# First query tile ahead of two value tiles, attention outputs split at their store

## The chip, the cores and the metric

The kernel runs on one core of a Trainium2 chip. A core has five engines that matter here, each working through its own instruction queue in order: TensorE (PE in the profile, with its weight loads as PEld), VectorE (DVE), ScalarE (ACT), GpSimd (POOL), and SyncE (SP), whose queue issues the DMA transfers. Engines wait for one another through semaphores; an instruction that waits holds back everything behind it on its engine. The metric is the device time of one launch in microseconds (us).

## The reference

A two-layer encoder over 1024 rows of 1024 values, all in float32. Layer 0 mixes rows by differential attention, layer 1 by multi-head latent attention; each layer has an adaptive shift, scale and gate from a vector c, a SiLU gate z on the branch, and an output projection added to x. What the change touches most is layer 0:

```python
def block(qb):
    sc = jnp.einsum('bqhcd,bkhcd->bhcqk', qb, k) * scale       # c: two score maps
    p = jax.nn.softmax(sc, axis=-1)
    p = p[:, :, 0] - lam * p[:, :, 1]
    return jnp.einsum('bhqk,bkhd->bqhd', p, v)

o = _from_blocks(lax.map(block, _to_blocks(q)))
o = _rmsnorm(o, subln_g) * (1.0 - lambda_init)
o = o.reshape(b, s, DA_WIDTH) * jax.nn.silu(z)
return o @ w_out
```

There are eight heads of 128 value columns. Both layers end with `x = x + gate * y`, and the trunk with an RMS norm.

## The kernel before

TensorE multiplies float32 matrices in a reduced format (fp32r), so every operand is held as a high part and a low part (`hi` is a cast, `lo` the difference), and `mm3` (lines 171 to 174) makes one product of three matmuls. The names end accordingly: `oth` and `otl`, `woh` and `wol`, `v_hl` with both.

Stages of layer 0, in order of time:

- Loading, normalising, the first half of the values, keys and queries of head 0 (0 to about 105 us).
- Strips of the gate z and eight **value tiles** (`v0_tile`), 24 matmuls each. Between them stand the adaptive vectors (`mod_dot` on DVE, weights in tiles `ada`). `store_v` evacuates a value tile from its PSUM bank: an ACT cast, a DVE difference, both into `v_hl` (two buffers), and a store to DRAM (`vS`).
- `attn0` for heads 0 to 7. A head has two halves of four **q tiles** of 128 rows. A q tile computes two score banks `s` (c = 0 and 1; two matmul pairs `qa`, `qb` each), for each a row maximum `nm` on DVE (line 351) and an exp on ACT (line 353), and then one combination on DVE (line 876). A q tile later its result `e` is transposed (`tr`), cast to `pth` and `ptl`, and multiplied with the values (`pv`). While PE would wait, `stream0.step` gives it strip steps of later heads' q, k and z (`acc`, three matmuls each): `FILL0` says how many of them stand at which point of a q tile, `FILL7` the same for head 7. There are 352 in all: `Z_PRE` of them ahead of attention, the rest in the loops.
- For each half of a head, `head_out` and `subln` apply the gate and the RMS norm: osq and o on ACT, ssq on PE, small 128x4 operations on DVE, the power on POOL (line 159), a product with `fin` on DVE (line 761). `finish` sends the row scale through DRAM to get it on all partitions (`bc_s`), multiplies o with it on POOL (line 726) and stores o to `oS` (line 727). The last half is kept and scaled on the spot by `tail0` (`rb`, line 733).
- In head 7, from q tile `Z_LAST` on, `extra0` loads what the output projection needs: for each head `load_ot` (lines 891 to 895: a DMA, an ACT cast, a POOL difference), and the weights (`OutW.load`, lines 917 to 921). `PRE0` places the projection's first steps.
- `out_proj` (about 708 to 860 us): `oacc` matmuls over heads, with the second halves' loads and `tail0` from the queue `side`.

Layer 1 repeats this with other attention (line 1294) from about 1010 to 1377 us, and its projection and the final norm end at 1475.

PSUM has eight banks. `psum(...)` closes one set of tags and opens another; `bank("acc", ...)` takes in turn the two lasting banks and those of the stage (`accx`, three in the stage of the value tiles, none in that of `attn0`, whose score tiles take two banks each). A scheduler then places every engine's instructions by its own cost model, so the order on an engine is not that of the code; `tc.issue_after` forces one instruction behind another.

Of the kernel before, what the change touches and what calls it, by code (L numbers as in the profile page):

```python
# [50 lines left out]
Z_LAST = 2  # L51
FILL7 = ((0, 1, 1, 1, 1, 1),) * 4
# [25 lines left out]
def trunk(ctx: ExitStack, tc: tile.TileContext, A, out):  # L78
# [45 lines left out]
    oS = [dr.tile([NH, 2, P, HF], F32, name=f"oS{l}") for l in range(2)]  # L124
# [15 lines left out]
    def part(name):  # L140
        lo, n = VEC[name]
        return vec[:, lo : lo + n]
# [7 lines left out]
    V.tensor_scalar(g8, part("subln_g"), 0.5 * (1.0 - LAM0) / GUARD, None, op0=ALU.mult)  # L150
# [160 lines left out]
    def store_v(l, sp, acc, tt, fh):  # L311
        v = sp.tile([P, 2, HF], F32R, name="v_hl", tag="vst", bufs=VB[l])
        S.copy(v[:, 0, :], acc)
        V.tensor_sub(v[:, 1, :], acc, f32v(v[:, 0, :]))  # L314
# [33 lines left out]
    def softmax_part(ap_, s_ps, zs):  # L348

        nm = sm.tile([P, 1], F32, name="nm")  # L350
        V.reduce_max(nm, s_ps, axis=AX.X, negate=True)  # L351
        e = ap_.tile([P, T], F32, name="e", tag="e", bufs=3) if ap_ else s_ps
        S.activation(e, s_ps, AF.Exp, bias=nm, scale=1.0, accum_out=zs)  # L353
        return e

    def bcast_rows(sp, y, tag, bufs):

        d_ = dr.tile([HF], F32, name="bc_d", tag="bcd", bufs=4)
        SP.dma_start(d_.rearrange("(p t) -> p t", p=P), y)
        b = sp.tile([P, HF], F32, name="bc_s", tag=tag, bufs=bufs)  # L360
        SP.dma_start(b, d_[None, :].to_broadcast([P, HF]))
        return b.rearrange("p (q t) -> p t q", t=4)
# [253 lines left out]
    def v0_tile(tt, fh, wv):  # L616
# [6 lines left out]
        store_v(0, p1b, acc, tt, fh)  # L623
# [93 lines left out]
    psum("ps2", sc=2, tr=1, pv=1)  # L717
# [4 lines left out]
    def finish(o, y, l, h, half, dst, ap_, dgs):  # L722

        if dst is None:
            rb = bcast_rows(ap_, y, "osq", 4)
            G.tensor_mul(t3(o), t3(o), rb)  # L726
            SP.dma_start(oS[l][h, half], o)
            return
# [16 lines left out]
    def subln(o, sq, zz, half, h, dst):  # L745
# [4 lines left out]
        def rest():  # L750
# [10 lines left out]
            V.scalar_tensor_tensor(out=y, in0=y, scalar=math.sqrt(P), in1=fin, op0=ALU.mult, op1=ALU.mult)  # L761
# [69 lines left out]
    def attn0(h, fills, extra=None, late=None):  # L831
# [11 lines left out]
        for qp in range(4):  # L843
            half = qp // 2
            if qp % 2 == 0:
                zz = sm.tile([P, 4], F32, name="zz")
            for t in range(2):
                ti = (qp * 2 + t) % 4
                ql = slice(ti * P, (ti + 1) * P)
                zs = [zz[:, ti : ti + 1], sm.tile([P, 1], F32, name="z1")]  # L850
                es = []
# [6 lines left out]
                def scores(c):  # L858
                    s_ps = bank("sc", "s", [P, T])
                    qa, qb = QS[h][half]  # L860
                    for src, fst in ((qa, True), (qb, False)):
                        for kc in range(2):
                            PE.matmul(s_ps[:, kc * HF : (kc + 1) * HF], src[:, c, ql], KS[h][kc][:, c, :], start=fst, stop=not fst)  # L863
                    es.append(softmax_part(None if c else a0b, s_ps, zs[c]))

                scores(0)
                fill(0)
                if tails[0]:
                    tails[0].turn(1)
                fill(1)  # L870
                scores(1)
                e0, e1 = es
                z0, z1 = zs
                V.reciprocal(z1, z1)
                V.tensor_scalar(z1, z1, z0, neglam[:, 0:1], op0=ALU.mult, op1=ALU.mult)
                V.scalar_tensor_tensor(out=e0, in0=e1, scalar=z1[:, 0:1], in1=e0, op0=ALU.mult, op1=ALU.add)  # L876
                fill(2)
                after_scores(fill, 3)
# [10 lines left out]
    for h in range(NH - 1):  # L889
        attn0(h, lambda i: FILL0[i % 2])  # L890
    def load_ot(l, dst, src):
        hi, lo = dst
        SP.dma_start(f32v(lo), src)
        S.copy(hi, f32v(lo))
        G.tensor_sub(lo, f32v(lo), f32v(hi))
        return hi, lo
# [105 lines left out]
    def extra0(i):  # L1002
# [3 lines left out]
        if i == Z_LAST:  # L1006
# [13 lines left out]
            ot = [lambda h=h: load_ot(0, OT[h][0], oS[0][h, 0]) for h in range(NH - 1)]  # L1020
# [25 lines left out]
    load_ot(0, OT[NH - 1][0], oS[0][NH - 1, 0])  # L1046
# [44 lines left out]
    side.add(None, None, tail0, *[lambda h=h: load_ot(0, OT[h][1], oS[0][h, 1]) for h in range(NH - 1)])  # L1091
# [29 lines left out]
    def lora(idx, dst, gvec, width, ws=None, first=None):  # L1121
# [21 lines left out]
        for half in range(2):  # L1143
# [6 lines left out]
            rb = bcast_rows(lr, y, "cbc", 1)  # L1150
# [101 lines left out]
    def attn1(h, fills, extra=None, late=None):  # L1252
# [50 lines left out]
        if late:  # L1303
            run_tails(lambda i: extra(8 + i))
            return ctx_["late"]
# [17 lines left out]
    ot = [lambda h=h: load_ot(1, OT1[h][0], oS[1][h, 0]) for h in range(NH - 1)]  # L1323
# [19 lines left out]
    load_ot(1, OT1[NH - 1][0], oS[1][NH - 1, 0])  # L1343
# [10 lines left out]
    side.add(None, None, tail1, *[lambda h=h: load_ot(1, OT1[h][1], oS[1][h, 1]) for h in range(NH - 1)])  # L1354
# [117 lines left out]
```

## Time and profile before

| what | us |
|---|---|
| median of 3 runs | 1482.54 (1481.86 to 1483.93) |
| profiled execution | 1477.0 |
| its span | 1475.0, mean granted TensorE clock 0.987 |
| stage of value tiles and first scores | 105 to 171 |
| attention, layer 0 | 156 to 708 |
| output projection, layer 0 | 708 to 860 |
| attention, layer 1 | 1010 to 1377 |

Rows of the profile read as follows. A timeline row has the start, the duration, the engine, the line, the operation, `out<-in` and the shape; `x2` means that two instructions are shown as one. In brackets stands the idle time of the engine before the instruction and what ended it. A group's row has the busy time of all its instructions, the mean of one in ns, and the idle time before them. A row of stretches has the busy time of PE, PEld, DVE, ACT and POOL with the number of instructions, then the TensorE clock that was granted (1.00 is full), the share of DMA engines busy, and GB/s.

### The profile page before, as it was taken

Reading aid. Unit: us, or ns where it says so; the run is one execution under the profiler, and the core shown is the slowest. Engines: PE = TensorE matmul, PEld = TensorE weight load, DVE = VectorE, ACT = ScalarE, POOL = GpSimd, SP = SyncE. Lnnn points to the kernel's source line nnn. Section 1 sums busy time; section 2 is a strip of 40 time slices with the busy share of each in tenths; the row PEclk is TensorE's granted clock in tenths of the full one; section 3 lists DMA queues with packets and bytes.
Section 4 is the critical chain, followed back from the end, with each engine's and each line's share of the span. In section 5 each row is a group of like instructions: output and inputs, shape, how many; then the busy total and the mean of one; then the engine's idle time right before and its main releaser. Section 6 shows DMA issues by size and latency. Waiting matters only on the chain.

```text
span 1475.0 us, 20427 instructions
## 1 busy us (share of the span) xinstructions
PE 1407.1 (95%) x7424; PEld 1169.7 (79%) x7424; DVE 856.9 (58%) x1286; ACT 710.9 (48%) x1256; POOL 605.9 (41%) x472
## 2 busy tenths in 40 slices
PE   5999799999999999998899999999999999999996
PEld 4777588888888888877787878877888888888885
DVE  6655777666676766677435435234655555555455
ACT  5622365656566656666343332225544454455342
POOL 4425163646454545545552254213122131232582
PEclk9999899999999999998999999999999999999999
DMA  9696723323222323243453126376222242261453
GB/s 332 218 270 202 252 65 93 78 88 86 87 77 82 84 81 100 61 139 116 164 171 125 40 65 217 127 210 187 74 69 88 81 110 70 58 200 58 156 163 138
DMA packets 119828, 187.45 MB, mean 127 GB/s; under 512 B 17328, under 2 KB 54320, under 8 KB 119728
## 3 DMA queue, kind: packets, MB, share of 16 engines
q1 hardware_dynamic: 119728, 186.16, 41.1%
q8 instruction: 58, 0.95, 0.3%
q14 instruction: 42, 0.34, 0.1%
HBM read 124.82 MB, written 37.70 MB: 110 GB/s over the span
## 4 chain that ended last, share of the span: by engine, by line
PE 68%; DMA 13%; DVE 7%; POOL 4%; ACT 3%; issue 3%; SPq 2%; POOLq 0%; ACTq 0%; DVEq 0%
PE s L1294 8%; PE acc L174 8%; PE acc L172 8%; PE acc L173 8%; PE s L863 7%; PE tr L334 7%; PE pv L173 4%; PE pv L172 4%; PE pv L174 4%; PE oacc L173 2%; PE oacc L172 2%; PE oacc L174 2%; DMA ada<-in_ada_g 2%; DMA wor<-in_w_out 2%; DMA wvr<-in_w_v 1%
## 5 line engine op out<-in xcount | busy, mean ns | idle before, releaser
L351 DVE TENSOR_REDUCE nm<-s 128x1 f32<-128x1024 f32 x192 | 233.8, 1219 | 71.9 <-PE s L863 64.8
L336 ACT CAST pth<-tr 128x512 fp32r<-128x512 f32 x256 | 150.2, 587 | 253.8 <-PE tr L334 252.0
L337 DVE TENSOR_TENSOR ptl<-tr,pth 128x512 fp32r<-128x512 f32 x256 | 176.1, 688 | 150.4 <-ACT pth L336 149.2
L199 POOL TENSOR_TENSOR wl<-wraw,wh 128x512 fp32r<-128x512 f32 (+2 forms) x94 | 115.1, 1226 | 278.6 <-ACT wh L198 250.4
L334 PE MATMUL tr<-ident,e 128*128 128x128 f32 x1024 | 155.9, 275 | 4.1 <-DVE ptl L337 3.5
L334 PEld LDWEIGHTS tr<-ident,e 128*128 128x128 f32 x1024 | 121.4, 141 | 46.3 <-DVE ptl L337 18.4
L353 ACT ACTIVATE e<-s,nm 128x1024 f32<-128x1024 f32 x128 | 143.3, 1120 | 23.3 <-DVE nm L351 22.7
L172 PE MATMUL acc<-h0h,wh 128*128 128x512 f32 x360 | 149.7, 416 | 0.5 <-DVE v_hl L314 0.5
L172 PE MATMUL pv<-pth,vt 128*128 128x256 f32 x512 | 147.6, 288 | 2.0 <-ACT pth L336 2.0
L173 PE MATMUL pv<-ptl,vt 128*128 128x256 f32 x512 | 146.7, 286 | 0.0
L174 PE MATMUL pv<-pth,vt 128*128 128x256 f32 x512 | 145.7, 285 | 0.0
L174 PE MATMUL acc<-h0h,wl 128*128 128x512 f32 x360 | 142.3, 395 | 0.0
L173 PE MATMUL acc<-h0l,wh 128*128 128x512 f32 x360 | 142.0, 395 | 0.0
L921 POOL TENSOR_TENSOR wol<-wor,woh 128x512 fp32r<-128x512 f32 x64 | 85.5, 1353 | 77.8 <-ACT woh L920 75.2
L172 PEld LDWEIGHTS pv<-pth,vt 128*128 128x128 f32 x512 | 98.3, 192 | 5.6 <-ACT pth L336 2.9
L173 PEld LDWEIGHTS pv<-ptl,vt 128*128 128x128 f32 x512 | 98.5, 192 | 2.9
L863 PE MATMUL s<-ks,qa 128*128 128x512 f32 x256 | 85.1, 414 | 14.6 <-ACT e L353 5.6
L174 PEld LDWEIGHTS pv<-pth,vt 128*128 128x128 f32 x512 | 98.4, 192 | 0.0
L198 ACT CAST wh<-wraw 128x512 fp32r<-128x512 f32 (+2 forms) x94 | 55.3, 589 | 84.9 <-PE acc L173 44.1
L726 POOL TENSOR_TENSOR o<-o,bc_s 128x512 f32<-128x512 f32 x30 | 46.4, 1547 | 120.7 <-DVE o L1264 94.2
L286 POOL TENSOR_TENSOR rp_sw<-rp_sw,sinT 128x512 f32<-128x512 f32 x42 | 55.2, 1314 | 80.4 <-DMA rp_sw<-rp_raw 79.5
L876 DVE SCALAR_TENSOR_TENSOR e<-s,z,e 128x1024 f32<-128x1024 f32 x64 | 82.0, 1281 | 1.5
(499 smaller groups left out, 3285.0 us busy)
## 6 DMA issues: line engine op xcount, KB each, us to landing
wraw<-in_w_s SPq DMA_DIRECT2D x76, 256.0 KB, 2.8
ada<-in_ada_ss SPq DMA_DIRECT2D x32, 512.0 KB, 5.8
vS<-v_hl SPq DMA_DIRECT2D x32, 512.0 KB, 5.6
vt<-vS SPq DMA_DIRECT2D x32, 512.0 KB, 3.6
wor<-in_w_out SPq DMA_DIRECT2D x64, 256.0 KB, 3.7
rp_sw<-rp_raw SPq DMA_DIRECT2D x168, 64.0 KB, 2.0
bc_s<-bc_d SPq DMA_DIRECT2D x34, 256.0 KB, 3.8
ada<-in_ada_g SPq DMA_DIRECT2D x16, 512.0 KB, 5.1
```

The costliest lines, as they stand in the source:

```text
L172: PE.matmul(psum, ah, bh, start=first, stop=False)
L173: PE.matmul(psum, ah, bl, start=False, stop=False)
L174: PE.matmul(psum, al, bh, start=False, stop=last)
L199: (V if pair_of else G).tensor_sub(l_[:, :n], raw[:, :n], f32v(h_[:, :n]))
L334: PE.transpose(tr[:, j, :], p[:, kt * P : (kt + 1) * P], ident)
L336: S.copy(pth[kh][:, :, dst], tr)
L337: V.tensor_sub(ptl[kh][:, :, dst], tr, f32v(pth[kh][:, :, dst]))
L351: V.reduce_max(nm, s_ps, axis=AX.X, negate=True)
L353: S.activation(e, s_ps, AF.Exp, bias=nm, scale=1.0, accum_out=zs)
L863: PE.matmul(s_ps[:, kc * HF : (kc + 1) * HF], src[:, c, ql], KS[h][kc][:, c, :], start=fst, stop=not fst)
L921: G.tensor_sub(lo, raw, f32v(hi))
L1294: PE.matmul(s_ps[:, kc * HF : (kc + 1) * HF], lhs, rhs(kc), start=i == 0, stop=i == 4)
```

## The change

1. `V_LATE = 6`: the first q tile of head 0 is computed ahead of value tiles 6 and 7 (`q_tile`, moved out of `attn0`). The PSUM set of attention opens there, so these two tiles have the two lasting banks only; their `v_hl` goes to the three `ada` buffers, where the others keep two.
2. `Z_PRE` 8 to 16: eight more strip steps ahead of the value tiles. `FILL0` has six steps in every q tile and five in the last; `Z_LAST` 2 to 4 and `FILL7`: head 7 has steps in four q tiles (4, 4, 4 and 1) instead of two (5 and 3), and its loads begin two q tiles later. `PRE0` is spread anew.
3. `finish` no longer stores o whole. A hook one q tile later splits it: an ACT copy into `bc_s`, a POOL difference in place, two stores. `oS` has both parts, and `load_ot` is two DMAs.
4. The row maximum of c = 0 is issued behind the combination of the q tile before.
5. The product with `fin` is on POOL; its factor sqrt(128) is in `g8`.
6. `tail0` comes behind three loads in `side` instead of ahead of them.

```diff
-FILL0 = ((1, 2, 1, 1, 1, 0), (1, 1, 1, 1, 1, 1))
+FILL0 = ((1, 2, 1, 1, 1, 0), (1, 1, 1, 1, 1, 1)) * 3 + ((1, 2, 1, 1, 1, 0), (1, 1, 1, 1, 1, 0))
-Z_PRE = 8
-PRE0 = (0, 0, 0, 0, 0, 0, 2, 0, 2, 1, 1)
+Z_PRE = 16
+V_LATE = 6
+PRE0 = (0, 0, 0, 0, 0, 0, 1, 1, 1, 2, 1)
-Z_LAST = 2
-FILL7 = ((0, 1, 1, 1, 1, 1),) * 4
+Z_LAST = 4
+FILL7 = ((0, 1, 1, 1, 1, 0),) * 4
-    V.tensor_scalar(g8, part("subln_g"), 0.5 * (1.0 - LAM0) / GUARD, None, op0=ALU.mult)
+    V.tensor_scalar(g8, part("subln_g"), 0.5 * (1.0 - LAM0) * math.sqrt(P) / GUARD, None, op0=ALU.mult)
...
-        store_v(0, p1b, acc, tt, fh)
+        if tt < V_LATE:
+            store_v(0, p1b, acc, tt, fh)
+        else:
+            store_v(0, pm, acc, tt, fh, "ada", 3)
...
+    def q_tile(h, half, ti, zz, ep, mid=lambda i: None):
+        ...
+        for c in range(2):
+            s_ps = bank("sc", "s", [P, T])
+            for src, fst in ((qa, True), (qb, False)):
+                for kc in range(2):
+                    PE.matmul(...)
+            with tc.issue_after(combined[-1]) if c == 0 and combined else nullcontext():
+                es.append(softmax_part(None if c else ep, s_ps, zs[c], 1 if ep is a0a else 3))
+            mid(c)
+        ...
+        combined.append(V.scalar_tensor_tensor(out=e0, in0=e1, scalar=z1[:, 0:1], in1=e0, op0=ALU.mult, op1=ALU.add).ins)
+        return e0
+
+    first, combined = [], []
     for tt in range(8):
-        next(mods_g)
+        if tt == V_LATE:
+            psum("ps2", sc=2, tr=1, pv=1)
+            zz0 = sm.tile([P, 4], F32, name="zz")
+            first += [zz0, q_tile(0, 0, 0, zz0, a0a)]
+        for _ in range(2 if tt < 5 else 1):
+            next(mods_g)
         v0_tile(tt, 1, wv1)
-        if tt < 5:
-            next(mods_g)
...
         if dst is None:
-            rb = bcast_rows(ap_, y, "osq", 4)
+            b, rb = bcast_rows(ap_, y, "osq", 4)
             G.tensor_mul(t3(o), t3(o), rb)
-            SP.dma_start(oS[l][h, half], o)
+
+            def split():
+                S.copy(b.bitcast(F32R), o)
+                G.tensor_sub(o.bitcast(F32R), o, b)
+                SP.dma_start(oS[l][h, half, 0], b)
+                SP.dma_start(oS[l][h, half, 1], o)
+
+            hooks.append(split)
             return
...
-            V.scalar_tensor_tensor(out=y, in0=y, scalar=math.sqrt(P), in1=fin, op0=ALU.mult, op1=ALU.mult)
+            G.tensor_mul(y, y, fin)
...
-    def load_ot(l, dst, src):
-        hi, lo = dst
-        SP.dma_start(f32v(lo), src)
-        S.copy(hi, f32v(lo))
-        G.tensor_sub(lo, f32v(lo), f32v(hi))
-        return hi, lo
+    def load_ot(dst, src):
+        for part_, src_ in zip(dst, src):
+            SP.dma_start(f32v(part_), src_)
...
-    side.add(None, None, tail0, *[lambda h=h: load_ot(0, OT[h][1], oS[0][h, 1]) for h in range(NH - 1)])
+    ot = [lambda h=h: load_ot(OT[h][1], [oS[0][h, 1, i] for i in range(2)]) for h in range(NH - 1)]
+    side.add(None, None, *ot[:3], tail0, *ot[3:])
```

How this stands on the engines at three places. First PE between the value tiles and the first scores. Before, the last of eight strip steps (`acc`) is followed by the scores of two q tiles without anything between:

```order
L174 MATMUL acc<-h0h_1_128,wl 128x512
L172 MATMUL acc<-h0h_1_132,wh 128x512
L173 MATMUL acc<-h0l_1_133,wh 128x512
L174 MATMUL acc<-h0h_1_132,wl 128x512
L863 MATMUL s<-ks,qa 128x512 x2
L863 MATMUL s<-ks,qb 128x512 x2
L863 MATMUL s<-ks,qa 128x512 x2
L863 MATMUL s<-ks,qb 128x512 x2
L863 MATMUL s<-ks,qa 128x512 x2
```

After it, with line numbers moved, the first q tile stands inside value tile 7 (`vps`), and 18 of that tile's matmuls follow:

```order
L175 MATMUL vps<-wvh,h0l_1_109 128x512
L720 MATMUL s<-ks,qa 128x512 x2
L720 MATMUL s<-ks,qb 128x512 x2
L720 MATMUL s<-ks,qa 128x512 x2
L720 MATMUL s<-ks,qb 128x512 x2
L173 MATMUL vps<-wvh,h0h_1_112 128x512
L174 MATMUL vps<-wvl,h0h_1_112 128x512
L175 MATMUL vps<-wvh,h0l_1_113 128x512
```

The second q tile's scores stand behind the rest of tile 7, and between its two score banks come eight strip matmuls.

Second, DVE in head 7. Before, where a row maximum `nm` stands ahead of the combination `e` of the q tile before:

```order
L337 TENSOR_TENSOR ptl<-tr,pth 128x4x128
L874 RECIPROCAL z_6544<-z_6544 128x1
L875 TENSOR_SCALAR z_6544<-z_6544,zz,neglam 128x1
L351 TENSOR_REDUCE nm<-s 128x1
L876 SCALAR_TENSOR_TENSOR e<-s,z_6544,e 128x1024
L337 TENSOR_TENSOR ptl<-tr,pth 128x4x128
```

And now, at a q tile of the same head:

```order
L727 TENSOR_SCALAR z_6458<-z_6458,zz,neglam 128x1
L728 SCALAR_TENSOR_TENSOR e<-s,z_6458,e 128x1024
L352 TENSOR_REDUCE nm<-s 128x1
L338 TENSOR_TENSOR ptl<-tr,pth 128x4x128
L662 SCALAR_TENSOR_TENSOR gz<-zth,acc 128x512
L352 TENSOR_REDUCE nm<-s 128x1
```

The combination is ahead of both maxima. This was so before in 53 of 64 q tiles, and is now in all.

Third, POOL at the first half's output of head 0 (`qb` are query combinations for head 1, `wl` the low parts of strip weights). Before:

```order
L286 TENSOR_TENSOR rp_sw<-rp_sw,sinT 128x512
L305 TENSOR_TENSOR qb<-rp_r,qa 64x512
L726 TENSOR_TENSOR o<-o,bc_s 128x512
L306 TENSOR_TENSOR qb<-rp_r,qa 64x512
L199 TENSOR_TENSOR wl<-wraw,wh 128x512 x2
```

And now:

```order
L796 TENSOR_TENSOR rq_y<-rq_y,sl_f 128x4
L287 TENSOR_TENSOR rp_sw<-rp_sw,sinT 128x512
L754 TENSOR_TENSOR o<-o,bc_s 128x512
L758 TENSOR_TENSOR o<-o,bc_s 128x512
L306 TENSOR_TENSOR qb<-rp_r,qa 64x512
L307 TENSOR_TENSOR qb<-rp_r,qa 64x512
L200 TENSOR_TENSOR wl<-wraw,wh 128x512 x2
```

The new product with `fin` (line 796) and the new difference (line 758) have come in. The difference stands right behind the product with the broadcast scale, and waits for ACT's copy (line 757); on ACT's queue that copy stands fourteen rows behind osq.

More of the change, by code (lines that the diff above doesn't have):

```diff
@@ L123, in trunk @@
     vS = [[dr.tile([4, 2, P, 2, 4, P], F32, name=f"vS{l}_{f}") for f in range(2)] for l in range(2)]
-    oS = [dr.tile([NH, 2, P, HF], F32, name=f"oS{l}") for l in range(2)]
+    oS = [dr.tile([NH, 2, 2, P, HF], F32, name=f"oS{l}") for l in range(2)]
     x1S = dr.tile([NT, P, D], F32, name="x1S")
@@ L309, in stack_q, with store_v @@
             SP.dma_start(f32v(t[0:64, 1, :]), f32v(t[64:128, 1, :]))
[L311 to L312 removed]
+    def store_v(l, sp, acc, tt, fh, tag="vst", bufs=None):
+        v = sp.tile([P, 2, HF], F32R, name="v_hl", tag=tag, bufs=bufs or VB[l])
         S.copy(v[:, 0, :], acc)
@@ L856, in fill, with mid @@
                         stream0.step(fl[i])
[L858 to L878, printed above, removed]
+                def mid(c):
+                    if c == 0:
+                        fill(0)
+                        if tails[0]:
+                            tails[0].turn(1)
+                        fill(1)
+                if first:
+                    e0 = first.pop()
+                else:
+                    e0 = q_tile(h, half, (qp * 2 + t) % 4, zz, a0b, mid)
+                    fill(2)
+                    after_scores(fill, 3)
                 side.tick()
```

40 lines of the change are left out of this document (23 added, 17 removed).

## The prediction, made before the changed kernel ran

> **What bounds the kernel now.** I read the page's busy shares and chain first, then the table of stretches, then the list of what TensorE waited for, and then the timelines of the places that these name.
>
> ```profile
> PE 1407.1 (95%) x7424; PEld 1169.7 (79%) x7424; DVE 856.9 (58%) x1286; ACT 710.9 (48%) x1256; POOL 605.9 (41%) x472
> PE 68%; DMA 13%; DVE 7%; POOL 4%; ACT 3%; issue 3%; SPq 2%; POOLq 0%; ACTq 0%; DVEq 0%
> 150.00:175.00 25.00, 15.91 (x59) 11.99 (x58) 18.36 (x28) 9.00 (x16) 2.52 (x2) 0.80 0.94 311
> 400.00:500.00 100.00, 99.13 (x553) 83.39 (x552) 70.55 (x105) 60.30 (x105) 55.25 (x44) 1.00 0.31 83
> 650.00:700.00 50.00, 42.35 (x242) 36.18 (x241) 38.03 (x57) 34.50 (x61) 27.61 (x22) 0.90 0.42 135
> 700.00:750.00 50.00, 45.21 (x208) 36.71 (x207) 16.97 (x25) 17.61 (x32) 31.21 (x25) 0.93 0.50 163
> 1400.00:1475.00 75.00, 62.48 (x291) 50.91 (x289) 44.38 (x106) 27.07 (x58) 41.88 (x31) 0.96 0.44 151
> ```
>
> A row of stretches gives length, busy time of PE, PEld, DVE, ACT and POOL, then granted clock, DMA share and GB/s. TensorE bounds the loops: 99.13 of 100 us at full clock. So nothing that the change does inside the loops can gain much there. What can be gained lies where PE stands idle or at a lower clock: behind the value tiles (150 to 175), in head 7 (650 to 700), and at the start of the output projection (700 to 750). The change edits all three.
>
> ```profile
> PE s L863 <- ACT e L353: 5.6, 4, 4.1
> PE s L863 <- DVE v_hl L314: 4.9, 1, 4.9
> PE s L863 <- DVE e L876: 4.0, 8, 2.1
> PE tr L334 <- DVE ptl L337: 3.5, 4, 1.6
> ```
>
> (Waits: total us, times, longest.) Few and long: one of 4.9 and one of 4.1 are at the first place, the 2.1 and the 1.6 at the second.
>
> **A. First q tile ahead of value tiles 6 and 7.** PE's timeline from the last value tile:
>
> ```profile
> 144.76 0.39 PE L172 MATMUL vps<-wvh,h0h 128*128 128x512 f32 x1
> 149.97 0.39 PE L174 MATMUL vps<-wvh,h0l 128*128 128x512 f32 x1
> 155.64 0.62 PE L863 MATMUL s<-ks,qa 128*128 128x512 f32 x2
> 156.10 0.62 PE L863 MATMUL s<-ks,qb 128*128 128x512 f32 x2
> 161.66 1.22 PE L863 MATMUL s<-ks,qa 128*128 128x512 f32 x2 [4.95 <-DVE v_hl L314]
> 162.68 1.05 PE L863 MATMUL s<-ks,qb 128*128 128x512 f32 x2
> 167.88 1.22 PE L863 MATMUL s<-ks,qa 128*128 128x512 f32 x2 [4.14 <-ACT e L353]
> 171.46 0.49 PE L172 MATMUL acc<-h0h,wh 128*128 128x512 f32 x1
> ```
>
> A value tile is 24 matmuls, 144.76 to 149.97 in 23 steps: 0.227 us each, 5.4 a tile. A pair of score matmuls follows the one before by 0.46 (155.64 to 156.10). From 155.64 to 171.46 PE issues eight pairs, 8 x 0.46 = 3.7 us of work in 15.8: 12.1 lost. Part of it is clock: after the gap, pairs stand 1.02 apart. The first wait is for a bank that a value tile's evacuation holds, and ACT's copies show why that is late:
>
> ```profile
> 151.05 0.59 ACT L313 CAST v_hl<-vps 128x512 fp32r<-128x512 f32 x1 [3.93 <-DMA vS<-v_hl]
> 155.85 0.59 ACT L313 CAST v_hl<-vps 128x512 fp32r<-128x512 f32 x1 [4.22 <-PE acc L174]
> 160.30 0.58 ACT L313 CAST v_hl<-vps 128x512 fp32r<-128x512 f32 x1 [3.36 <-DMA vS<-v_hl]
> vS<-v_hl SPq DMA_DIRECT2D x32, 512.0 KB, 5.6
> ```
>
> These are tiles 5, 6 and 7. Each waits until the store of the tile two before it has landed (5.6 us from issue), so the banks come free one in about 4.5 us, and the last only at 161.6. Now 18 value matmuls (4.1 us) stand between the first tile's scores and the second's, and tiles 6 and 7 have three buffers. The second z half, moved ahead, costs PE nothing net: 8 steps of 3 x 0.227 = 0.68. I count what remains. PE would be done with tile 5 at 149.97 + 5.4 - 2 x 5.4 = 144.5. Tile 6 wants tile 3's bank; its copy ran two spacings before tile 5's, near 142.1, but tile 0's store now stands behind the query swaps, and one spacing later, with 0.7 for the two evacuating instructions, it is 147.3: up to 2.8; the second score bank pair wants tile 5's (copy 151.05, or one spacing of 4.5 later): up to 1.7; the second q tile wants the first exp: about 1. That is 5.5, in pieces, instead of 12.1: **6.6 gained**. Range 0 (everything one store later) to 10 (2 left).
>
> Clock, from the same rows: after 4.95 and 4.14 idle the pairs slowed; in head 7, below, the pair after 2.07 idle did not. The Trainium skill, TensorE: Matmul & The Clock Gate, section Why this matters for your kernels, says to leave TensorE no idle gap over about 3 us. By that rule pieces of 2.8 and less keep full clock, and the 6.6 stands. But the row 650 to 700 shows 0.90 with no gap over 2.1, so pieces can add up; by that the gain would be about 2 smaller.
>
> **B. Head 7.** Rows of ACT, DVE and PE, and the two groups of casts:
>
> ```profile
> 671.90 0.62 ACT L894 CAST oth<-otl 128x512 fp32r<-128x512 f32 x1 [0.81 <-DMA otl<-oS]
> 672.01 1.22 DVE L351 TENSOR_REDUCE nm<-s 128x1 f32<-128x1024 f32 x1 [0.41 <-PE s L863]
> 673.15 1.27 DVE L876 SCALAR_TENSOR_TENSOR e<-s,z,e 128x1024 f32<-128x1024 f32 x1
> 674.48 0.74 PE L863 MATMUL s<-ks,qa 128*128 128x512 f32 x2 [2.07 <-DVE e L876]
> 675.06 0.63 PE L863 MATMUL s<-ks,qb 128*128 128x512 f32 x2
> 679.96 0.82 PE L334 MATMUL tr<-ident,e 128*128 128x128 f32 x4 [1.60 <-DVE ptl L337]
> L894 ACT CAST oth<-otl 128x512 fp32r<-128x512 f32 x8 | 5.0, 619 | 4.8 <-DMA otl<-oS 4.6
> L895 POOL TENSOR_TENSOR otl<-otl,oth 128x512 fp32r<-128x512 f32 x8 | 10.2, 1281 | 20.5 <-ACT oth L894 19.6 <-DMA wor<-in_w_out 0.9
> ```
>
> In the stretch 650 to 700 PE misses 7.65 us idle and, at 0.90, up to 5.0 more: 12.7. Three edits meet here. (1) Fillers: head 7 keeps 13 strip steps in four q tiles instead of 8 in two; five more x 0.68 = 3.4 us of work moves from loops where PE is full into tiles where it waits. (2) ACT no longer stops, in order, for arriving outputs: most of the eight oth casts of 0.62 and some of the seven ot_h ones, and the waits before them (4.6 in all); two copies of 0.62 come in. POOL loses as many subtractions of 1.28. (3) The reduction at 672.01 ran ahead of the combination, which released the scores at 674.48: behind it, those start about 1.2 earlier, and the reduction's exp about as much later. In DVE's order it ran ahead so in 11 of 64 q tiles, four of them here. Not all can go: a bare tile holds DVE for two reductions, a combination and two P casts of 0.69 (ptl), some 5.1 us, and two and a half tiles stay bare. I take **6**: the 3.4, and a third of the other 9.3. Range 1 to 10.
>
> Z_LAST also delays the loads: they begin after q tile 4, not 2. Fourteen output loads and seven weights of 256 KB, 5.5 MB, then fit into three tiles only at near 270 GB/s; before it was 135 here. That is a rival below.
>
> **C. Start of the projection.** The last head's scale:
>
> ```profile
> 710.73 5.05 POOL L921 TENSOR_TENSOR wol<-wor,woh 128x512 fp32r<-128x512 f32 x4 [5.33 <-ACT woh L920]
> 715.89 1.01 POOL L159 TENSOR_TENSOR rq_y<-sl_w,mhalf 128x4 f32<-128x4 f32 x1
> 716.93 1.21 DVE L761 SCALAR_TENSOR_TENSOR rq_y<-rq_y,sl_f 128x4 f32<-128x4 f32 x1 [1.12 <-POOL rq_y L159]
> 718.62 2.04 PE L733 MATMUL rb<-sq,ones 128*128 128x128 f32 x8 [3.26 <-DVE sq L732]
> L761 DVE SCALAR_TENSOR_TENSOR rq_y<-rq_y,sl_f x16: 144/164/1284, 218.5 to 716.9; 128x4 f32<-128x4 f32 x16
> ```
>
> (The last row gives min, median and max in ns.) PE waited 3.26 us, and the pair rows of A show what such a gap does after it: eight matmuls in 2.04, which I count as 1 us too long. The chain from ssq to rb stays as long as it is, since six matmuls stand between in both; what goes is contention. Beside POOL's four weight splits the DVE product took 1.21, of its usual 0.16; 18 matmuls later POOL has done those. The product on GpSimd is an instruction that no row shows; its nearest is the power, 1.01 at the same size, so it costs 0.16 (as on DVE) to 1.01; I take 1.0. That gives back 1.2 of contention on DVE (L761's excess 1.05, and some of its neighbours'), loses nothing further against 1.21, and shortens the gap to about 2.2, with the slow matmuls gone: **2 gained**, range 0 to 3. By the Trainium skill, GPSIMD Engine Reference, section 4.1 Engine selection, a two-input elementwise operation belongs on VectorE, GpSimd being about twice slower. The medians agree (0.16 on DVE, 1.01 for POOL's power), and by them alone C would gain 0.8 less; the 1.21 on this path speaks the other way.
>
> **Loops, and the end.** Fifteen outputs a layer are split in the loops: 30 ACT copies of 0.62 and 30 subtractions of 1.28, the same number as are taken out, and 30 stores and 30 loads of 256 KB more. The row 400 to 500 shows ACT 60.3, POOL 55.3 and DMA 0.31 busy under a full PE, which hides them, unless ACT must wait inside its queue (rival 3). The small product off DVE frees at most (1.28 - 0.16) where it was held. I take **0**, range -4 to +2. For the final projection (row 1400 to 1475) seven casts and subtractions go, but its last weights are still issued behind the output stores: 0, range 0 to 3.
>
> Sum: 6.6 + 6 + 2 + 0 = 14.6. Against the profiled execution, span 1475.0 of 1477.0 us, that is a span near 1460.4. That execution was 5.5 below the runs' median of 1482.54, so the median should come to 1482.5 - 14.6 = **1468**.
>
> **Rivals.** *1. The wait behind the value tiles only moves.* Three fewer banks serve tiles 6 and 7, and tile 0's store goes behind query swaps; the stores landing every 4.5 us then hold PE as long as before. For it: every one of the three copies waited. Against: 4.1 us of matmuls stand in between now. A gives 0: 1482.5 - 8 = 1474.5.
>
> *2. Head 7 stays slow, on transfers.* The 5.5 MB in three tiles need some 20 us at 270 GB/s, of about 23 there; the four added outputs' stores share them. For it: ACT at 671.90 already waited for an output. Against: the casts no longer sit in ACT's queue while they come. B gives 0: 1482.5 - 8.6 = 1474.
>
> *3. Slower: the split holds ACT.* Rows of the first half's output:
>
> ```profile
> 207.56 0.60 ACT L742 ACTIVATE osq<-pv 128x512 f32<-128x512 f32 x1 [2.00 <-PE pv L174]
> 225.01 1.54 POOL L726 TENSOR_TENSOR o<-o,bc_s 128x512 f32<-128x512 f32 x1
> L727 SPq DMA_DIRECT2D oS<-o x13: 319/320/326, 226.6 to 640.0; - x13
> L337 DVE TENSOR_TENSOR ptl<-tr,pth 128x512 fp32r<-128x512 f32 x256 | 176.1, 688 | 150.4 <-ACT pth L336 149.2
> ```
>
> The product with the broadcast scale ended at 226.6, 19 us behind osq. The copy stands fourteen ACT rows behind osq, of twenty-eight per half head. Thirteen stores in 413.4 us make 34.4 a half head, so the copy comes about 17 behind osq. ACT could come 2 us early and hold, with the exps, and the P casts that the DVE casts of the last row wait for, queued behind it; POOL's subtraction stands right behind the product and holds the query combinations as well. At 30 outputs, an exposed 0.5 us each is 15 us, which eats the gains; that is the point from which it decides. With 1 us each: 1482.5 - 14.6 + 30 = 1498. Against: ACT is idle for 40 us in 100, and fillers stand between a tile's scores and its use. An exposed 0.7 gives 1489.
>
> *4. The edits don't do what they say:* banks hold tile 6, so the first tile's scores come no earlier than the stores allow, and casts were not what held head 7. Only C's 2 is left: 1480.5.
>
> **Numbers.** Forecast 0.53; rival 1 0.13, rival 2 0.12, rival 3 0.13, rival 4 0.09. The forecast, 1 and 2 are faster by over 0.2% (3 us, about what a measurement here can tell from no change): 0.78. Rival 4 lies within it: 0.09. Rival 3 is slower: 0.13. The forecast's own range is 1460 to 1473. For 8 in 10, all lower ends together (10 + 10 + 3 + 2 + 3 = 28) would give 1455, hardly all at once, so 1458; above, rivals 1, 2 and 4 lie inside, and 1484 leaves out most of rival 3.
>
> **What would show it.** A: in PE's timeline two score pairs ahead of the last 18 value matmuls, no wait over 3 us and a clock above 0.95 in the 25 us around them; a wait of 4 or more for v_hl says rival 1. B: at least 46 busy in the 50 us of head 7, no combination waited for; waits of projection matmuls for loaded outputs or weights, at a DMA share over 0.8, say rival 2. C: the wait before rb near 2.2. Loops: PE at 99 or more in 100; a drop below 98.5, with ACT's copy waiting for POOL, says rival 3. My forecast is wrong if the time lies above 1474 or below 1460, most likely through A or B, which carry 12.6 of the 14.6.

## The result, and the profile after

The changed kernel takes 1521.93 us (median of 4 runs, 1520.43 to 1524.47); the kernel before, on the same chip, 1482.88. The ratio is 1.0265, 95% interval [1.0247, 1.0283]: 39 us slower, where 14.6 us faster was forecast. Its profiled execution took 1521.2 us with a span of 1519.4, so 44 us more than the one before (1475.0).

Busy shares and chain, from the page of the kernel after:

```profile
PE 1421.1 (94%) x7424; PEld 1175.5 (77%) x7424; DVE 852.2 (56%) x1270; ACT 710.0 (47%) x1256; POOL 608.0 (40%) x488
PE 55%; DMA 13%; POOL 9%; DVE 8%; ACT 6%; issue 5%; SPq 3%; POOLq 0%; ACTq 0%; DVEq 0%
```

ACT and POOL have no more work than they had: their busy times are within 2.1 us of those before. But PE's share of the chain fell from 68% to 55%, and POOL's and ACT's rose from 4% and 3% to 9% and 6%. The time went into waiting for short operations of these two. The table of stretches, kernel after, shows where:

```profile
150.00:175.00 25.00, 23.40 (x103) 18.36 (x102) 19.28 (x30) 9.16 (x16) 2.65 (x3) 1.00 0.88 288
400.00:500.00 100.00, 95.95 (x519) 79.44 (x520) 71.89 (x98) 58.61 (x106) 56.42 (x47) 0.98 0.32 85
500.00:600.00 100.00, 92.97 (x506) 78.30 (x505) 63.91 (x92) 54.40 (x97) 46.60 (x38) 0.97 0.32 88
650.00:700.00 50.00, 42.12 (x234) 35.15 (x233) 34.56 (x50) 25.84 (x47) 16.07 (x15) 0.93 0.46 140
1200.00:1300.00 100.00, 93.33 (x559) 78.99 (x558) 49.63 (x67) 47.73 (x88) 25.93 (x21) 1.00 0.29 87
```

and of the kernel before, for layer 1's attention:

```profile
1200.00:1300.00 100.00, 99.22 (x598) 84.61 (x597) 53.59 (x71) 49.39 (x90) 24.41 (x19) 1.00 0.29 85
```

The stretch behind the value tiles is what was hoped for: 23.4 of 25 busy at full clock, against 15.9 at 0.80. Everything else that the forecast counted on staying full is not: in the stretches of 100 us shown here, PE is busy for 93 to 96, where it was above 99. That is the sign which the prediction named for its rival 3.

To price stages against each other I took PE's matmuls in pairs and summed how much later each began than the median step of its shape (0.231 us for 512 columns, 0.120 for 256, 0.109 for a transpose). This counts idle time and slow clock together, in us, from the profiled execution of each kernel (one run; that of the kernel before was 6 us below its median, so differences of a few us here are not certain). Head 7 counts up to its last score matmul:

```
stage                               before   after   ACT's copy later
up to 100 us                          11.5    13.9    11.7
value tiles                            0.5     1.6     2.7
first two q tiles                     12.2     2.1     2.0
rest of heads 0 to 6                   5.8    28.8    11.0
head 7                                13.7    15.8    10.0
projection 0 to scores of layer 1     13.7    16.0    14.4
attention, layer 1                    10.2    35.9    15.0
the rest                               6.2     4.9     5.1
sum                                   73.8   119.0    71.9
```

(The last column is an experiment below.) The change gained 10.1 us behind the value tiles and lost 23.0 in the loops of layer 0 and 25.7 in those of layer 1. The waits of the kernel after name the carrier, first PE's (total us, times, longest), then those of ACT, POOL and DVE:

```profile
PE tr L335 <- DVE ptl L338: 39.0, 31, 3.2
PE s L720 <- DVE v_hl L315: 1.3, 1, 1.3
```

```profile
ACT bc_s L757 <- POOL o L754: 98.2, 30, 6.6
```

```profile
POOL o L754 <- DMA bc_s<-bc_d: 49.8, 11, 7.8
```

```profile
DVE rp_r L290 <- POOL rp_sw L287: 50.1, 23, 7.6
```

ACT's 30 new copies waited 98.2 us inside ACT's queue for POOL's product with the broadcast scale, 3.3 each; PE's wait for `ptl` rose from 3.5 us in 4 waits to 39.0 in 31. One of the longest, in the timelines of the kernel after (POOL, ACT, DVE and PE, in order of time):

```profile
538.81 1.55 POOL L754 TENSOR_TENSOR o<-o,bc_s 128x512 f32<-128x512 f32 x1 [5.03 <-DMA bc_s<-bc_d]
540.39 0.62 ACT L757 CAST bc_s<-o 128x512 fp32r<-128x512 f32 x1 [3.67 <-POOL o L754]
541.09 1.29 POOL L758 TENSOR_TENSOR o<-o,bc_s 128x512 fp32r<-128x512 f32 x1 [0.73 <-ACT bc_s L757]
542.34 1.29 POOL L287 TENSOR_TENSOR rp_sw<-rp_sw,sinT 128x512 f32<-128x512 f32 x1
543.66 1.76 DVE L290 TENSOR_TENSOR rp_r<-rp_r,rp_sw 128x512 f32<-128x512 f32 x1 [5.11 <-POOL rp_sw L287]
545.46 0.62 ACT L297 CAST ks<-rp_r 64x512 fp32r<-64x512 f32 x1 [3.92 <-DVE rp_r L290]
546.74 0.59 ACT L337 CAST pth<-tr 128x512 fp32r<-128x512 f32 x1
548.10 0.82 PE L335 MATMUL tr<-ident,e 128*128 128x128 f32 x4 [3.16 <-DVE ptl L338]
```

POOL reaches the product before the scale has landed and waits 5.03. ACT has reached the copy and waits 3.67; POOL then waits 0.73 for the copy, subtracts, and only then makes the rotary product `rp_sw` of a later head, for which DVE waits 5.11 and ACT another 3.92. Behind those two stands `pth`, whose transposes were long done, and PE waits 3.16 for `ptl`. A chain of three in-order engines runs through one output, which the projection reads more than 100 us later.

### The profile page after: what moved, and what is told of

Its sections match the earlier page's. It is cut to its first block, busy times and chain, and to the rows that moved or that the text cites. A ratio compares the mean times of both kernels' runs of the same rounds, so it can differ in the third digit from the quotient of the medians.

```text
span 1519.4 us, 20529 instructions
## 1 busy us (share of the span) xinstructions
PE 1421.1 (94%) x7424; PEld 1175.5 (77%) x7424; DVE 852.2 (56%) x1270; ACT 710.0 (47%) x1256; POOL 608.0 (40%) x488
## 4 chain that ended last, share of the span: by engine, by line
PE 55%; DMA 13%; POOL 9%; DVE 8%; ACT 6%; issue 5%; SPq 3%; POOLq 0%; ACTq 0%; DVEq 0%
PE acc L173 6%; PE acc L175 6%; PE acc L174 6%; PE s L1315 6%; PE tr L335 5%; PE s L720 5%; PE oacc L174 3%; PE oacc L173 3%; PE oacc L175 3%; DMA bc_s<-bc_d 3%; POOL o L754 3%; PE pv L174 2%; PE pv L173 2%; PE pv L175 2%; DMA vS<-v_hl 2%
## 5 line engine op out<-in xcount | busy, mean ns | idle before, releaser
L335 PE MATMUL tr<-ident,e 128*128 128x128 f32 x1024 | 159.2, 279 | 39.4 <-DVE ptl L338 39.0
L728 DVE SCALAR_TENSOR_TENSOR e<-s,z,e 128x1024 f32<-128x1024 f32 x64 | 82.2, 1284 | 2.2
```

The costliest lines, as they stand in the source:

```text
L335: PE.transpose(tr[:, j, :], p[:, kt * P : (kt + 1) * P], ident)
```

## Experiments

Three theories at first. S: ACT's copy waits in its queue for POOL's product, and what is queued behind reaches PE late. N: the forced order of the row maximum delays exps and casts, which the wait for `ptl` would show as well. D: the added 15.7 MB of transfers make the scale late. All ratios below are to the kernel before, run on the same chip between the runs, with 95% intervals.

**The split undone**, the rest of the change kept:

```diff
-            def split():
...
-            hooks.append(split)
+            SP.dma_start(oS[l][h, half, 0], o)
...
     def load_ot(dst, src):
-        for part_, src_ in zip(dst, src):
-            SP.dma_start(f32v(part_), src_)
+        hi, lo = dst
+        SP.dma_start(f32v(lo), src[0])
+        S.copy(hi, f32v(lo))
+        G.tensor_sub(lo, f32v(lo), f32v(hi))
```

> The changed kernel with the split alone undone: outputs are stored whole again, and loads cast and subtract as before. Theory S (ACT's copy waits in its queue for POOL's product, 98.2 us in 30 waits, and the P casts behind it reach PE late): the loops are full again, 1465 to 1475, with ACT's total wait for POOL's product at 0 and PE's wait for ptl back near 4 us. Rival N (the forced order of the row maximum delays exps and casts): 1510 or more, ptl wait stays near 39. Rival D (15.7 MB of added transfers make the scale broadcast late): as S.

Measured: 1484.95 us, ratio 1.0015 [0.9998, 1.0032]. Of the loss of 39 us, 37 go with the split, and N falls. But S expected 10 to 20 us less than this: the rest of the change is no gain of its own.

**The split alone**, on the kernel before (the same edit the other way).

> The kernel before with the split alone added. Theory S: slower than before by more than the change was, since the gain of about 10 us at the value tiles is missing: 1520 to 1535. Rival N: about 1483, as the forced order isn't in it. Rival D: as S.

Measured: 1512.82 us, ratio 1.0198 [1.0160, 1.0237]. So the split costs 30 us by itself there, less than I expected. Its ACT waits for the product:

```profile
ACT bc_s L729 <- POOL o L726: 82.7, 30, 4.0
```

Layer 1 loses 35.0 us below cadence (10.2 before, 35.9 in the changed kernel), the rest of heads 0 to 6 19.9 (5.8 and 28.8). So the split alone costs 24.8 us in layer 1 and 14.1 in heads 0 to 6, 39 together, or 1.3 a copy. (The times show 30 of these: head 7 lost 3 less here, and the profiled execution of the kernel before was 6 below its median.) The copies wait 2.2 us on average in layer 0 and 3.3 in layer 1.

**ACT's copy queued one q tile later.** The same copies, subtractions and transfers; only their place in ACT's queue differs. The scheduler moves an instruction up when its model says that the input is ready, so the copy is tied behind an exp of the later q tile:

```diff
+    exps = []
...
     def softmax_part(ap_, s_ps, zs, bufs=3):
...
-        S.activation(e, s_ps, AF.Exp, bias=nm, scale=1.0, accum_out=zs)
+        exps.append(S.activation(e, s_ps, AF.Exp, bias=nm, scale=1.0, accum_out=zs).ins)
...
             def split():
-                S.copy(b.bitcast(F32R), o)
+                with tc.issue_after(exps[-1]):
+                    S.copy(b.bitcast(F32R), o)
...
-            hooks.append(split)
+            hooks.append(lambda f=split: hooks.append(f))
```

> The changed kernel, with the same split and the same transfers, but ACT's copy is queued one q tile (about 8 us) later, behind an exp of that tile, so that POOL's product is done when ACT reaches it. Theory S: ACT's wait before the copy falls from 98.2 us to under 10, and the time to 1465 to 1480. Rival D: transfers are the same, so the time stays at 1515 to 1525. Rival N: 1515 to 1525.

Measured: 1475.29 us, ratio 0.9944 [0.9925, 0.9963]: 47 us less than the changed kernel, and faster than the kernel before. Its waits, ACT's, POOL's, DVE's and PE's, and two stretches of its loops:

```profile
ACT bc_s L760 <- POOL o L756: 2.8, 1, 2.8
```

```profile
POOL o L761 <- ACT bc_s L760: 97.4, 26, 8.4
POOL o L756 <- DMA bc_s<-bc_d: 48.6, 11, 7.8
```

```profile
DVE rp_r L290 <- POOL rp_sw L287: 47.9, 22, 7.7
PE tr L335 <- DVE ptl L338: 9.0, 10, 2.0
```

```profile
500.00:600.00 100.00, 98.39 (x552) 83.05 (x551) 69.14 (x101) 58.76 (x103) 48.30 (x41) 1.00 0.32 90
1200.00:1300.00 100.00, 98.02 (x590) 83.62 (x590) 52.81 (x70) 50.03 (x92) 29.52 (x23) 1.00 0.34 95
```

This settles S and excludes D: the scale lands as late as in the changed kernel (48.6 us of waits against 49.8), the transfers are the same, and ACT's 98.2 us of waits are down to 2.8. POOL now has them instead, 97.4 us for ACT's copy, and that costs little: DVE waits for rotary products as it did (47.9 against 50.1), but PE's wait for `ptl` is down from 39.0 to 9.0. The wait was moved from an engine through which PE's path runs to one beside it.

**The forced order of the row maximum taken out** of the changed kernel (the `issue_after` around `softmax_part` gone).

> The changed kernel without the forced order of the row maximum behind the combination. Theory S: 1522 within 4. Rival N: 1470 to 1485. Rival D: 1522 within 4.

Measured: 1520.91 us, ratio 1.0255 [1.0231, 1.0278]. The order is not the cause.

**The split kept out of layer 1**, with ACT's copy later in layer 0.

> The run with ACT's copy queued later, with the split in layer 0 only; layer 1 stores whole outputs and casts them when loaded. Layer 1 lost 19.7 us below cadence from 1000 to 1400 in that run, 11.7 without the split; the final projection 1 against 5. If the split is a net cost in layer 1: 1469 to 1473. If the casts in the final projection cost as much: 1474 to 1478.

Measured: 1475.57 us, ratio 0.9938 [0.9923, 0.9953], the same as with both layers split. In its trace layer 1's loops lose 12.7 us instead of 15.0, and the part behind them under 1 us more, so the casts there do not cost as much as the loops gain; a difference this small is not told by the times.

**The split with the later copy on the kernel before.**

> The kernel before with the split alone, ACT's copy queued one q tile later. The same split without that delay made the kernel before 29.7 us slower. If the wait in ACT's queue is all of it: 1476 to 1486, with ACT's wait before the copy under 10 us. If the copies, subtractions and transfers cost of themselves: 1495 or more.

Measured: 1481.36 us, ratio 0.9985 [0.9968, 1.0002]. Without the wait the split costs nothing measurable, and by itself gains nothing measurable: ACT had no wait for POOL's product left, POOL has it.

```profile
POOL o L733 <- ACT bc_s L732: 104.9, 30, 8.4
```

What is left to explain is why the rest of the change, without the split, is worth nothing, though PE gained 10 us at one place. In the trace of that run (7 us above its median) heads 0 to 6 lose 14.8 us against 5.8 before, and 26.1 against 13.7 go between the last scores of head 7 and the first of layer 1. The following runs price parts of the change. The first was a surprise.

**Part 1 alone** (first q tile ahead, second z half ahead; the rest as before, except that the product with fin stays a plain one on DVE, and that head 7 has 6 strip steps left instead of 8).

> Of the change only part 1 and the second z half ahead of the value tiles: no split, no forced order of the row maximum, product with fin on DVE, tail0 ahead of the loads, head 7 and its loads planned as before. If the 10 us that PE's timeline gained behind the value tiles (12.1 us below its cadence before, 2.1 to 2.4 in the kernels with the change) stand alone: 1472 to 1475. If they are given back later: 1479 to 1484.

Measured: 1509.16 us, ratio 1.0167 [1.0136, 1.0198], slower by 24 us where both guesses had it faster or the same, though the first two q tiles lost only 2.0 us below cadence. Heads 0 to 6 lost 41.2. PE's waits, and a stretch of DVE and PE:

```profile
PE s L720 <- DVE e L728: 23.5, 19, 1.4
```

```profile
211.06 1.24 DVE L789 TENSOR_TENSOR rq_y<-rq_y,sl_f 128x4 f32<-128x4 f32 x1 [0.94 <-POOL rq_y L160]
212.22 1.27 DVE L728 SCALAR_TENSOR_TENSOR e<-s,z,e 128x1024 f32<-128x1024 f32 x1
213.55 0.73 PE L720 MATMUL s<-ks,qa 128*128 128x512 f32 x2 [1.35 <-DVE e L728]
```

The 128x4 product stands ahead of a combination in DVE's queue, waits 0.94 for POOL's power, then takes 1.24, and the combination frees the score bank 2.2 us later than it could. PE waited 1.35 us for it in 13 of the 19 places, about twice a head.

**The same with the product on POOL.**

> The run of part 1 alone with the product with fin on POOL. If the product on DVE, ahead of a combination, made that run's loss in the loops (41 us below cadence): 1488 to 1494, PE's wait for combinations under 10 us. If the order of the row maximum did: 1505 to 1510.

Measured: 1491.47 us, ratio 1.0058 [1.0038, 1.0077]. PE's wait for combinations is 4.5 us in 5. So some 16 of the 24 us (1.0167 to 1.0058) were the product's place, and heads 0 to 6 lost 24.3 instead of 41.2; the order of the row maximum, as free as in the run before, was not the cause of these. **With the later copy and the product on DVE**:

```diff
-            G.tensor_mul(y, y, fin)
+            V.tensor_mul(y, y, fin)
```

> The same run with the product with fin on DVE again. In the run of part 1 alone that product stood ahead of a combination in DVE's queue, waited 0.94 us for POOL's power and then took 1.24, and PE waited 23.5 us in 19 places for combinations. If it is this product: 1488 to 1500, with that wait back. If that run was slow for another reason: 1474 to 1478.

Measured: 1484.36 us, ratio 1.0013 [0.9996, 1.0030], against 0.9944: part 5, the smallest edit, is worth about 0.7%, some 10 us. It is less than I expected; PE's wait for combinations is 8.9 us in 12, against 2.4 in 5.

**Head 7 and its loads as before**, without the split:

```diff
-FILL0 = ((1, 2, 1, 1, 1, 0), (1, 1, 1, 1, 1, 1)) * 3 + ((1, 2, 1, 1, 1, 0), (1, 1, 1, 1, 1, 0))
+FILL0 = ((1, 2, 1, 1, 1, 0), (1, 1, 1, 1, 1, 1)) * 4
-PRE0 = (0, 0, 0, 0, 0, 0, 1, 1, 1, 2, 1)
+PRE0 = (0, 0, 0, 0, 0, 0, 2, 0, 2, 1, 1)
-Z_LAST = 4
-FILL7 = ((0, 1, 1, 1, 1, 0),) * 4
+Z_LAST = 2
+FILL7 = ((0, 1, 1, 1, 1, 1),) * 4
```

> The run without the split, with head 7 and its loads planned as before as well (loads from q tile 2, strip steps in two q tiles). If the later loads are what cost that run its gain (33 us below cadence from 600 to 750, against 22 before): 1471 to 1477. If the forced order, the product on POOL or tail0's place cost it: 1482 to 1487. Against the run of part 1 alone it also prices these three.

Measured: 1492.05 us, ratio 1.0045 [1.0027, 1.0063]. Both guesses missed: the plan of head 7 as before made it slower. In its trace 25.6 us are lost in heads 0 to 6, against 14.8. It doesn't differ from the run with part 1 and the product on POOL (1.0058, intervals overlap), so the forced order and tail0's place bring nothing measurable there. **The same on the run with the later copy**:

> The run with ACT's copy queued later, with head 7 and its loads planned as before. In that run transfers filled the DMA engines in head 7 (share 1.01 from 665 to 675) and a weight cast of ACT waited 3.46 us for its load, with an exp behind it. If the squeezed loads cost: 1469 to 1473. If covering two more q tiles is worth more than that: 1477 to 1481.

Measured: 1491.32 us, ratio 1.0042 [1.0026, 1.0058], 16 us more than with the new plan; both guesses missed again. The loss is not in head 7 (11.5 us below cadence against 10.0) but in heads 0 to 6 (24.2 against 11.0), once in each head. **Only the strip steps per head**, 48 for 47 (the first pair of lines of the last diff alone; as the total is fixed, head 7 then has 6 steps instead of 13):

> The run with ACT's copy queued later, with six strip steps in the last q tile of a head instead of five (48 a head instead of 47), head 7 and its loads as in the change. The run with all of head 7's plan as before lost 13 us more than this one in heads 0 to 6 and 1.5 more in head 7. If the count of strip steps a head makes that loss: 1487 to 1492. If the plan of head 7 and its loads makes it: 1474 to 1478.

Measured: 1489.69 us, ratio 1.0039 [1.0016, 1.0063]. So it is the count of strip steps: heads 0 to 6 lost 22.3 us, head 7 11.2. With that count, head 7's plan and its later loads change nothing that can be told (1.0042 and 1.0039). What happens once a head there, in DVE's and ACT's timelines:

```profile
476.74 0.69 DVE L290 TENSOR_TENSOR rp_r<-rp_r,rp_sw 128x512 f32<-128x512 f32 x1 [3.17 <-POOL rp_sw L287]
477.46 0.62 ACT L297 CAST ks<-rp_r 64x512 fp32r<-64x512 f32 x1 [3.52 <-DVE rp_r L290]
478.75 0.58 ACT L337 CAST pth<-tr 128x512 fp32r<-128x512 f32 x1
```

A rotary product arrives late, DVE and ACT wait for it in their queues, and `pth` behind them. With 48 steps DVE's wait for that product, 2.8 to 3.9 us, stands 40 to 42 us into each of heads 1 to 6, and each of them loses 2.5 to 4.3 us. With 47 it stands there in head 1 alone, and waits of about 3 us for it come at other points of heads 3, 5 and 6; heads 1, 5 and 6 lose 2.6, 1.9 and 3.3 us, the others 1.4 or less. That the strips drift by one step a head with 47, and stand still with 48, would explain it, but which step is unlucky was not tried; the kernel before also has 48 and does not lose (5.8 us).

Three edits priced singly on the run with the later copy. **The first q tile behind all value tiles again:**

```diff
-V_LATE = 6
+V_LATE = 8
...
-        if tt == V_LATE:
-            psum("ps2", sc=2, tr=1, pv=1)
...
+    psum("ps2", sc=2, tr=1, pv=1)      # behind the loop over value tiles
+    zz0 = sm.tile([P, 4], F32, name="zz")
+    first += [zz0, q_tile(0, 0, 0, zz0, a0a)]
```

> The run with ACT's copy queued later (1475.3), with the first q tile behind all eight value tiles again; the rest stays. It prices part 1 alone: if the 10 us that PE's timeline shows at that place are a real gain, 1483 to 1487. If the eight strip steps ahead cover the wait as well, 1474 to 1478.

Measured: 1475.55 us, ratio 0.9944 [0.9927, 0.9962]: no difference at all. The scheduler here put 17 of the strip matmuls ahead of the first scores, 10 ahead of the second q tile's and 11 between its two banks, and the place lost 1.5 us instead of 12.2. So strip matmuls between the first scores remove the wait as value matmuls do; the kernel before had its 24 ahead of them in one piece.

**The forced order taken out:**

> The same run without the forced order of the row maximum, which then stands ahead of the combination in 15 of 64 q tiles. If the order matters once the split doesn't hide it: 1479 to 1490. If it doesn't: 1474 to 1478.

Measured: 1475.71 us, ratio 0.9941 [0.9923, 0.9958]: nothing, though the maximum stands ahead of the combination in 15 of 64 q tiles.

**tail0 ahead of the three loads:**

> The same run with tail0 ahead of the three loads, as before. PE's wait before rb was 1.9 us in it against 3.3 before. If that is what the place buys: 1476 to 1479, with the wait at 3 or more. If nothing: 1474 to 1476.

Measured: 1479.02 us, ratio 0.9969 [0.9955, 0.9982]. The wait before rb is 3.3 us again, against 1.9. The intervals overlap, so 1.4 us is shown in the trace, and the rest of the 3.7 is not.

The version with the later copy beats both kernels, by 0.56% [0.37, 0.75] the kernel before; no variant of it was clearly better.

## Why the prediction was wrong

**The step that failed** is the paragraph on the loops: "I take **0**, range -4 to +2". The traces lost 23.0 us more in the rest of heads 0 to 6 and 25.7 more in layer 1, 49 together. Some 39 of these are the split's: so much it cost when put on the kernel before, 1.3 a copy, and so much the later place in ACT's queue took back. The other 9, in heads 0 to 6, stand in the trace without the split too. The counting of copies and transfers was right, and it was the wrong thing to count. The work is hidden, as the paragraph said, "unless ACT must wait inside its queue", and that became the result: rival 3, to which I gave 0.13 and which my range left out.

Rival 3 had mechanism, place and form of price right, and its size too small: its largest price was 1 us a copy. I put ACT about 2 us ahead of the product's end, from rows of layer 0. For layer 0 of the kernel before with the split alone that was so: 2.2 on average, with the product's end 19 us behind osq, as read, and some 1.0 a copy lost. Two things were missing. I looked at no row of layer 1, where the copies waited 3.3 on average and cost 1.7 each. And the order changed: in layer 0 of the changed kernel the product ended as late as before (16.5 to 22.4 behind osq, 18.6 in the middle), but ACT came to the copy 13 to 18 behind it, 16 in the middle, and waited 3.2. POOL came to the product ahead of the scale (49.8 us in 11 waits, against 9.6 in 3 before), and the rotary product was held with it:

```profile
POOL o L726 <- DMA bc_s<-bc_d: 9.6, 3, 5.6
```

For cover I relied on ACT's idle 40 in 100, an average. ACT is as idle in the changed kernel (710.0 us busy, 710.9 before), and still of the 3.3 us that a copy waited some 1.3 came through to PE. The 0.7 exposed that I had as an example would have been 21 us; it was 1.3, 39.

**A second step failed: the sum of the gains, 14.6.** Without the split the change is at 1.0015, no gain. So rival 3's 1498 was short of the measured 1522 by 24 us, about 9 from the price of a copy and about 15 from gains that did not come. A's gain came in the trace and was given back later, in heads 0 to 6 and between head 7's last scores and layer 1; what takes it there without the split, no run singles out.

**A**, predicted 6.6 with a range to 10, measured 10.1: the longest wait is now 1.3, the first scores of the kernel after:

```profile
154.93 0.62 PE L720 MATMUL s<-ks,qa 128*128 128x512 f32 x2
157.33 0.72 PE L720 MATMUL s<-ks,qa 128*128 128x512 f32 x2 [1.32 <-DVE v_hl L315]
163.81 0.50 PE L173 MATMUL acc<-h0h,wh 128*128 128x512 f32 x1 [0.28 <-DVE v_hl L315]
```

I had counted a wait of 2.8 for tile 3's bank that did not come. The clock stayed at 1.00 in the row 150 to 175. That agrees with the rule of the Trainium skill quoted there (TensorE: Matmul & The Clock Gate, Why this matters for your kernels), as far as one place can. Another place differs from it. In the run with the later copy one gap of 2.02 us stands behind 6 us in which PE was busy throughout, and about 1 us after it the clock was 0.50 for some 3 us:

```profile
690.00:696.40 6.40, 6.40 (x37) 5.10 (x36) 4.69 (x8) 2.90 (x5) 1.40 (x1) 1.00 0.91 286
698.46 0.66 PE L335 MATMUL tr<-ident,e 128*128 128x128 f32 x4 [2.02 <-DVE ptl L338]
699.50:702.50 3.00, 3.00 (x11) 2.42 (x10) 0.69 (x1) 0.24 (x1) 0.00 (x0) 0.50 0.72 185
```

So a gap under 3 us is not always safe here. Yet the first q tile was not needed for A's gain: strips did as well (so rival 1 was wrong too). One row of A was read wrongly: for tile 6 the profile names an `acc` matmul, not a store, as what ended ACT's wait.

**B**, predicted 6: in the changed kernel head 7 lost 15.8 instead of 13.7, and 10.0 with the later copy. But this ends at the last score; up to the last `pv` it is 14.2 before, 19.9 in the changed kernel and 13.9 with the later copy, so next to nothing was gained. One copy still waits there, the 2.8 us for the last output stored in layer 0; `pth` stands behind it, and PE waits the 2.02 named above. Rival 2's transfers did show in the run with the later copy:

```profile
665.00:675.00 10.00, 5.94 (x26) 4.39 (x25) 6.08 (x10) 5.07 (x11) 4.40 (x4) 0.86 1.01 362
670.27 0.62 ACT L943 CAST woh<-wor 128x512 fp32r<-128x512 f32 x1 [3.46 <-DMA wor<-in_w_out]
672.04 1.15 PE L722 MATMUL s<-ks,qa 128*128 128x512 f32 x2 [2.63 <-ACT e L356]
```

All DMA engines are busy, at 362 GB/s, ACT waits 3.46 for a weight, and an exp behind it costs PE 2.63. I had this as a bandwidth of 270 over three tiles; it came in one burst, in which PE was busy for 5.94 of 10 us. The prices of the loads' start and of the fillers within head 7 were not separated further: with 48 strip steps a head they change nothing measurable together, and without the split they were not tried apart from the strip count.

**C**, predicted 2 with a gap of 2.2: the gap was 1.9 (1.4 less) and the eight matmuls behind it took 1.13 instead of 2.04, 2.3 together, as the row of the kernel after shows:

```profile
743.30 1.13 PE L768 MATMUL rb<-sq,ones 128*128 128x128 f32 x8 [1.91 <-DVE sq L767]
```

The product with fin, which I priced at 1.0, took 0.2 (below). I missed where this edit matters: not here, but in the loops, where a product waiting on DVE holds a combination, worth 10 us. And the strip count, which I treated as work moved from one place to another, is worth 14; the traces show late rotary products with it, and that these make the whole of it is argued. Both are of the same kind as the step that failed: what is queued behind a waiting instruction.

## What to carry to other kernels

An instruction that is free by its duration is priced by when its input comes and by what stands behind it in its engine's queue: write both times down, in the order after the change, and add the wait on the engine that feeds the bottleneck, not its idle share. If such work can be late, tie it behind something later, or put it on an engine whose queue the critical path does not pass; here that turned 39 us slower into 8 us faster with the same work. And price small moves in a kernel with a scheduler one at a time, since the order that they cause is worth more than they are.

## What was not expected of the hardware

GpSimd's 128x4 product takes a fifth of its 128x4 power at the same size, and never varied:

```profile
L796 POOL TENSOR_TENSOR rq_y<-rq_y,sl_f x16: 201/202/204, 213.2 to 741.7; 128x4 f32<-128x4 f32 x16
```

(min, median, max in ns; the power took 1007.) On VectorE, with the factor in the same instruction, it took 144 to 1284 ns in the kernel before. What decides is whether a GpSimd instruction is already running. In that kernel, in part 1 alone and in the run with the product back on DVE there are 24 such products over 900 ns: each began 25 to 325 ns inside a GpSimd instruction and ended 16 to 25 ns behind it. The other 24 took 144 to 165; 22 of them began with GpSimd idle, two 5 ns behind the start of an instruction. In part 1 alone 15 of 16 were slow, as the product there followed POOL's power, behind which POOL went straight on. The Trainium skill's preference for VectorE (GPSIMD Engine Reference, section 4.1 Engine selection) holds for the medians, 164 against 202 ns, at much less than twice; for the largest, 1284 against 204, it is the other way round.
